# The front of a hybrid decoder step: where the squares of the first norm are summed, and the order of the first adaLN and weight loads

## The chip, the cores and the metric

The kernel runs on one core of one Trainium2 chip. The metric is the device time of one execution in microseconds (us); lower is better. The core's engines are TensorE (PE, matrix products), VectorE (DVE), ScalarE (ACT), GpSimd (POOL), and SyncE (SP), which issues most of the transfers between HBM and the on-chip memory. Each engine works off its own list of instructions in order, and they wait for each other by semaphores. Between SBUF (the on-chip memory) and PE's accumulators lies PSUM.

## The reference

One step of a trunk of two layers: an SSD (Mamba-2) layer, then a pooling layer, each with adaLN modulation, an RMS norm ahead and a residual add. 1024 prompt tokens and 8 x 8 sample tokens go through it together, 1088 tokens in all, in float32. What the change touches is the beginning: the norm and modulation of the first layer, and its first input projection.

```python
def rmsnorm(x, g):
    xf = x.astype(jnp.float32)
    return xf * lax.rsqrt(jnp.mean(xf * xf, axis=-1, keepdims=True) + EPS) * g.astype(jnp.float32)
...
    sc = jax.nn.silu(c.astype(jnp.float32))
    for i in range(DEPTH):
        mod = sc @ ada_w[i].astype(jnp.float32) + ada_b[i].astype(jnp.float32)
        shift, scale, gate = jnp.split(mod, 3, axis=-1)
        hn = (rmsnorm(x, norm_g[i]) * (1.0 + scale[:, None]) + shift[:, None]).astype(x.dtype)
        ...
    zxbcdt = h @ w_in
    z = zxbcdt[..., :D_INNER]
    xbc = zxbcdt[..., D_INNER:D_INNER + CONV_DIM].astype(jnp.float32)
    dt_raw = zxbcdt[..., D_INNER + CONV_DIM:].astype(jnp.float32)
```

## The kernel before

Activations lie transposed: channels on the 128 partitions, tokens along the free axis. So `x` is eight tiles `xs[k]` of 128 x 1088, one for each 128 of the 1024 channels. A row of up to 512 numbers fits one PSUM buffer, so tokens are cut into the three chunks of `CH`: 368, 368 and 352.

To keep float32 accuracy with fast products, a value is kept as a rounded `hi` and a rest `lo`, and a product is three: hi x hi, hi x lo, lo x hi (`mm1`, L189: L190, L191, L192). Products on unrounded float32 operands, such as those with the tile `ones`, are issued as one plain product.

The front (`setup` and `front`) does this:

- `setup` issues the loads on SP's queue: `ct` (the conditioning), the eight `x` tiles, then the constants `vec` and `kc`. It forms silu(c) in `scp`. `warm(62)` (L241 to L245) puts 62 products of `ones` by `ones` on PE, whose results nobody reads.
- `front` squares each `xs[k]` on ACT (L1403, L1407) into one of four `raw` buffers, and DVE adds the squares in `rst` (L1408). `ms_log` (L298) sums over the partitions, one product of `ones` (128 x 128) by a chunk of `rst` (L302), and takes the logarithm on ACT (L305, Ln); `rstd` (L318, Exp with -0.5) gives the inverse root.
- An adaLN step `ada_first(kt)` gives shift and scale of one channel tile. `ada_block` (L248) loads its slab of 1 MB in two halves (L257), multiplies it with `scp` in eight small products, four at a time side by side in strips of the array (L261, two records each), copies the result with ACT to `mp` (L266) and turns it with two products (L270); two DVE pieces (L280, L281) then give `shf` and `scl`.
- The first two column blocks of the input weights are loaded whole (`stream_raw`, L121) and split whole: ACT rounds 128 x 1024 numbers (L141), DVE forms the rest (L145).
- The loop over k: `modulate` (L320) scales `xs[k]` on DVE (L325), ACT adds the shift and rounds (`hh`, L331), DVE forms the rest (`hl`, L332), ACT adds the shift in place for the time-step projection (L333); the 64 sample tokens take five more small pieces. For k = 0 this goes in three chunks. Then PE has 18 products (two weight blocks, three chunks, three products each) in six open accumulators, and four strip products for `pdt` (L1443) with `wdt`. The adaLN steps 1 to 7 run inside the loop, two ahead.

After the loop `front` drains the accumulators, and the rest of the first projection follows (`wh`, `wl` are its split weights), then the pairs of blocks, the scan and the second layer.

The kernel is written in a framework with a scheduler: when the program is built, it merges what the Python code issues into one list for each engine by its own estimate of readiness. `keep_in_program_order` and `issue_after(i)` bind it: an instruction issued within `issue_after(i)` is not put ahead of `i`. Tiles of one tag share `bufs` buffers in turn, and the framework adds the waits. `Slots` hands out large SBUF buffers, which also hold the adaLN slabs.

Of the kernel before, what the change touches and what calls it, by code (L numbers as in the profile page):

```python
# [15 lines left out]
P = 128  # L16
# [83 lines left out]
class Build:  # L100
# [87 lines left out]
    def mm1(self, ps, w, k, act, ch, first, last):  # L188
        nc, (hi, lo), (ah, al), (a, n) = self.nc, w, act, ch  # L189
        nc.tensor.matmul(ps[:, :n], hi[:, k, :], ah[:, a:a + n], start=first, stop=False)  # L190
        nc.tensor.matmul(ps[:, :n], hi[:, k, :], al[:, a:a + n], start=False, stop=False)  # L191
        nc.tensor.matmul(ps[:, :n], lo[:, k, :], ah[:, a:a + n], start=False, stop=last)  # L192
# [9 lines left out]
    def setup(self):  # L202
# [4 lines left out]
        for k in range(8):  # L207
            t = self.slots.get("x")
            nc.sync.dma_start(t, io["xT"][k])
            self.xs.append(t)  # L210
        self.vec = cp.tile([P, V_N], F32, tag="vec", name="vec")
        nc.sync.dma_start(self.vec, io["vec"])
        self.kc = cp.tile([P, K_N], F32, tag="kc", name="kc")
        nc.sync.dma_start(self.kc, io["kc"])
        self.ident = self.kc[:, K_ID:K_ID + 128]
        self.ones = cp.tile([P, P], F32, tag="ones", name="ones")
        nc.vector.memset(self.ones, 1.0)

# [7 lines left out]
        self.warm(62)  # L226
# [12 lines left out]
        nc.gpsimd.memset(self.ctm, 0.0)  # L239

# [7 lines left out]
    def ada_block(self, src):  # L248
# [3 lines left out]
        for hh in range(2):  # L252
            if src is None:
                raws.append(self.stream_next_raw().rearrange("p a m -> p (a m)"))
            else:
                raws.append(self.slots.get("ada"))
                nc.sync.dma_start(raws[hh][:, :1024].rearrange("p (a b) -> p a b", a=4), src[:, 4 * hh:4 * hh + 4, :])  # L257
# [8 lines left out]
        nc.scalar.activation(mp, pm[:, :256], AF.Copy)  # L266
# [53 lines left out]
    def modulate(self, l, k, x, rst, hi, lo, a, n, t):  # L320
# [4 lines left out]
        nc.vector.scalar_tensor_tensor(out=t[:, :pn], in0=x[:, a:a + pn], scalar=self.scl[l][:, k, 8:9], in1=rst[:, a:a + pn], op0=ALU.mult, op1=ALU.mult)  # L325
# [4 lines left out]
        else:  # L330
            nc.scalar.activation(hi[:, a:a + pn], t[:, :pn], AF.Identity, bias=sh)  # L331
            last = nc.vector.scalar_tensor_tensor(out=lo[:, a:a + pn], in0=t[:, :pn], scalar=sh, in1=hi[:, a:a + pn].bitcast(F32), op0=ALU.add, op1=ALU.subtract)  # L332
            nc.scalar.activation(t[:, :pn], t[:, :pn], AF.Identity, bias=sh)  # L333
        if pn < n:
# [3 lines left out]
            eng.tensor_tensor(out=t[:, pn:n], in0=x[:, s], in1=rst[:, s], op=ALU.mult)  # L338
# [118 lines left out]
    def dt_phase(self, ps):  # L457
# [15 lines left out]
        nc.scalar.activation(an, self.vec[:, V_ALOG:V_ALOG + 1], AF.Exp)  # L473
        nc.vector.tensor_scalar(an, an, -1.0, None, op0=ALU.mult)
# [919 lines left out]
    def front(self):  # L1394

        nc, io, sl = self.nc, self.io, self.slots
        xs = self.xs
        wdts = sl.get("wdt")
        wdt = wdts[:, :256].rearrange("p (k m) -> p k m", k=8)
        nc.sync.dma_start(wdt, io["wdt"])  # L1400
        rst = sl.get("rst")
        with self.ln_set():
            nc.scalar.activation(rst, xs[0], AF.Square)  # L1403
            for k in range(1, 8):
                sq = self.raw_tile()
                for a, n in CH if k == 7 else ((0, TOK),):
                    nc.scalar.activation(sq[:, a:a + n], xs[k][:, a:a + n], AF.Square)  # L1407
                    nc.vector.tensor_tensor(out=rst[:, a:a + n], in0=rst[:, a:a + n], in1=sq[:, a:a + n], op=ALU.add)  # L1408
            for a, n in CH:
                self.ms_log(rst, rst, a, n, 1.0 / 1024, "mm", 3)  # L1410
                self.rstd(rst[:, a:a + n])
        self.ada_first(0)
        self.hn = []

        self.wslots = []
        lower = [self.stream_split(i, True) for i in range(2)]
        with self.tc.issue_after(self.sel):
            self.warm(8, "mm", 3)
        self.ada_first(1)
        ws = [self.wsplit.pop(i) for i in range(2)]  # L1420
# [3 lines left out]
        pdt = self.pp.tile([P, 512], F32, tag="tr", bufs=2, name="pdt")  # L1424
        for k in range(8):
            if k < 6:
                self.ada_first(k + 2)
            if k == 4:
                self.stream_split(2)
            if k == 6:  # L1430
                self.stream_split(3)
            hi, lo = sl.get("hh", F32R), sl.get("hl", F32R)
            for a, n in CH if k == 0 else ((0, TOK),):
                last = self.modulate(0, k, xs[k], rst, hi, lo, a, n, xs[k][:, a:a + n])
                if lower:
                    lower.pop(0)()
            self.hn.append((hi, lo))
            for i in range(2):
# [509 lines left out]
```

## Time and profile before

| | |
|---|---|
| time, median of 3 runs | 1591.16 us (1591.13 to 1593.46) |
| the profiled execution | 1591.15 us |
| its span, first to last instruction | 1589.0 us |
| records of instructions in it | 30720 |
| mean granted PE clock | 0.999 |

The profile is one execution. A record is one piece of work of an engine; a plain float32 product leaves two. A row of the timeline gives the start and length in us, the engine, the line of the kernel, the operation, what it writes and reads, shapes, the number of records merged in the row, and in brackets the idle time before it with what ended it. A row of a line's own view gives the least, median and largest length in ns, and the first and last start. In a row of stretches stand start and end, length, then for each engine its busy time and records, then the clock granted to PE, the share of the DMA engines and the GB/s. In the view of waits a row gives who waited for whom, the sum in us, the count and the longest.

### The profile page before, as it was taken

What the parts mean: (1) busy time and instruction counts of PE and PEld (TensorE: products, weight loads), DVE (VectorE), ACT (ScalarE), POOL (GpSimd) and SP (SyncE); (2) the same over time, 40 slices, a digit from 0 to 9 for tenths busy, and PEclk for the clock granted to TensorE, in tenths of its full rate; (3) what the DMA queues carried; (4) which work ended last, traced back from release to release, by engine and by line L of the source; (5) the groups of instructions that cost most, each with busy time, mean ns of one, the idle gap of its engine ahead of it and who ended that gap; (6) DMA issues with size and microseconds to landing.
All of it is one profiled execution on the core that took longest, in us unless ns stands there. A gap on an engine that the chain in (4) does not pass through costs nothing.

```text
span 1589.0 us, 30720 instructions
## 1 busy us (share of the span) xinstructions
PE 1568.2 (99%) x11946; PEld 1505.1 (95%) x11946; DVE 1301.7 (82%) x2152; ACT 790.1 (50%) x1512; POOL 525.5 (33%) x558
## 2 busy tenths in 40 slices
PE   9999999999999999999999999999999999999997
PEld 7899999999999999989999999999999999999997
DVE  6874889887899989889888858988889777667886
ACT  6663344466766666665456348433333233233373
POOL 0133456522331413141211232366666530000241
PEclk9999999999999999999999999999999999999999
DMA  9422232365555565679999432232333379565783
GB/s 356 167 101 101 80 112 84 111 194 173 161 179 165 162 209 167 212 259 297 311 332 320 164 127 69 85 121 100 117 115 115 104 250 365 140 180 178 163 172 117
DMA packets 122304, 275.57 MB, mean 173 GB/s; under 512 B 18192, under 2 KB 59312, under 8 KB 122160
## 3 DMA queue, kind: packets, MB, share of 16 engines
q1 hardware_dynamic: 118128, 260.90, 48.4%
q0 software_dynamic: 4032, 12.72, 4.7%
q8 instruction: 94, 1.54, 0.4%
q14 instruction: 50, 0.41, 0.1%
HBM read 201.12 MB, written 70.23 MB: 171 GB/s over the span
## 4 chain that ended last, share of the span: by engine, by line
PE 85%; DVE 6%; issue 3%; DMA 3%; ACT 2%; POOL 1%; SPq 0%; DVEq 0%; ACTq 0%; POOLq 0%
PE st L1070 11%; PE st L1072 11%; PE st L1071 11%; PE mm L190 10%; PE mm L191 10%; PE mm L192 10%; PE op L1289 2%; PE op L1291 2%; PE op L1290 2%; PE y L641 2%; PE S L619 2%; PE y L645 1%; PE am L261 1%; PE tr L580 1%; PE tr L577 1%
## 5 line engine op out<-in xcount | busy, mean ns | idle before, releaser
L1072 PE MATMUL st<-hh,w 128*128 128x272 f32 x832 | 240.2, 289 | 0.0
L1070 PE MATMUL st<-hh,w 128*128 128x272 f32 x832 | 240.0, 288 | 0.0
L1071 PE MATMUL st<-hl,w 128*128 128x272 f32 x832 | 240.0, 288 | 0.0
L1070 PE MATMUL st<-t,w 128*128 128x272 f32 x624 | 179.6, 288 | 0.0
L1072 PE MATMUL st<-t,w 128*128 128x272 f32 x624 | 179.5, 288 | 0.0
L1071 PE MATMUL st<-t,w 128*128 128x272 f32 x624 | 179.2, 287 | 0.0
L190 PE MATMUL mm<-hh,wh 128*128 128x368 f32 (+1 forms) x528 | 178.9, 339 | 0.0
L191 PE MATMUL mm<-hl,wh 128*128 128x368 f32 (+1 forms) x528 | 174.0, 330 | 0.0
L192 PE MATMUL mm<-hh,wl 128*128 128x368 f32 (+1 forms) x528 | 173.2, 328 | 0.0
L1070 PEld LDWEIGHTS st<-hh,w 128*128 128x128 f32 x832 | 156.7, 188 | 0.0
L1071 PEld LDWEIGHTS st<-hl,w 128*128 128x128 f32 x832 | 156.7, 188 | 0.0
L1072 PEld LDWEIGHTS st<-hh,w 128*128 128x128 f32 x832 | 156.5, 188 | 0.0
L182 ACT ACTIVATE w<-wr 128x512 fp32r<-128x512 f32 x104 | 64.9, 629 | 165.5 <-PE st L1072 134.2
L627 POOL TENSOR_TENSOR hd<-h,cd 128x256 f32<-128x256 f32 x56 | 46.1, 824 | 285.9 <-DVE h L628 135.6
L1289 PE MATMUL op<-b,w 128*128 128x272 f32 x448 | 129.4, 289 | 0.0
L1290 PE MATMUL op<-b,w 128*128 128x272 f32 x448 | 128.8, 287 | 0.2 <-DVE b L1218 0.2
L1291 PE MATMUL op<-b,w 128*128 128x272 f32 x448 | 128.9, 288 | 0.0
L190 PE MATMUL mm<-gh,wh 128*128 128x368 f32 (+1 forms) x372 | 125.3, 338 | 0.0
L192 PE MATMUL mm<-gh,wl 128*128 128x368 f32 (+1 forms) x372 | 122.4, 329 | 0.0
L191 PE MATMUL mm<-gl,wh 128*128 128x368 f32 (+1 forms) x372 | 122.2, 328 | 0.1
L1070 PEld LDWEIGHTS st<-t,w 128*128 128x128 f32 x624 | 117.6, 189 | 0.1
L1072 PEld LDWEIGHTS st<-t,w 128*128 128x128 f32 x624 | 117.3, 188 | 0.0
(310 smaller groups left out, 4596.9 us busy)
## 6 DMA issues: line engine op xcount, KB each, us to landing
wr<-win SPq DMA_DIRECT2D x48, 512.0 KB, 3.8
wr<-pin SPq DMA_DIRECT2D x32, 512.0 KB, 3.8
acb<-acd SPq DMA_DIRECT2D x60, 256.0 KB, 4.4
wr<-pout SPq DMA_DIRECT2D x28, 512.0 KB, 5.2
x<-x1d SPq DMA_DIRECT2D x24, 544.0 KB, 6.7
x1d<-x SPq DMA_DIRECT2D x22, 544.0 KB, 6.2
wr<-pout POOLq DMA_DIRECT2D x20, 512.0 KB, 6.0
x<-xT SPq DMA_DIRECT2D x16, 544.0 KB, 6.7
```

What stands on the lines that cost most here:

```text
L182: self.last_hi = self.nc.scalar.activation(hi, src, AF.Copy)
L190: nc.tensor.matmul(ps[:, :n], hi[:, k, :], ah[:, a:a + n], start=first, stop=False)
L191: nc.tensor.matmul(ps[:, :n], hi[:, k, :], al[:, a:a + n], start=False, stop=False)
L192: nc.tensor.matmul(ps[:, :n], lo[:, k, :], ah[:, a:a + n], start=False, stop=last)
L619: nc.tensor.matmul(S[:, 256 * i:256 * i + 256], Bt, xde.rearrange("p r q -> p (r q)"), start=True, stop=True)
L627: nc.gpsimd.tensor_tensor(out=hd, in0=h[-1], in1=cd.unsqueeze(2).to_broadcast([P, 4, 64]), op=ALU.mult)
L1070: nc.tensor.matmul(ps[c][:, :QUART], hi[:, k], xh[:, t], start=(k == 0), stop=False)
L1071: nc.tensor.matmul(ps[c][:, :QUART], hi[:, k], xl[:, t], start=False, stop=False)
L1072: nc.tensor.matmul(ps[c][:, :QUART], lo[:, k], xh[:, t], start=False, stop=(k == 3))
L1289: nc.tensor.matmul(ps[:, :QUART], hi[:, k], xh, start=k == 0, stop=False)
L1290: nc.tensor.matmul(ps[:, :QUART], hi[:, k], xl, start=False, stop=False)
L1291: nc.tensor.matmul(ps[:, :QUART], lo[:, k], xh, start=False, stop=k == 7)
```

## The change

Five things are done in the front, and nothing elsewhere.

1. The squares are no longer added on DVE. For each tile, PE multiplies `ones` with the three chunks of its squares and accumulates over the eight tiles in three PSUM buffers (`ms`). After each of the first seven sets of three products come three filling products, and the filling ahead of them is 48 instead of 62.
2. SP's loads stand in another order: the slab of adaLN step 0 ahead of the constants, then `kc`, `vec`, the first halves (k below 4) of the two first weight blocks, slab 1, the second halves, `wdt`, and the other slabs.
3. The first adaLN step stands behind the last set of sums in PE's list; Ln and Exp of the second and third chunk, and the splits, stand behind its `mp`.
4. The two first weight blocks are split in parts of 2, 2 and 4 of the eight k (`first_split`).
5. In the loop, k = 1 also goes in chunks, k = 0 takes its products chunk by chunk, the shift in place of x tiles 0 and 1 is moved behind an adaLN step of k = 1 (L1492), the `pdt` products of k = 0 go with those of k = 1, and the adaLN steps are placed by hand among the products.

PE's list at the beginning, before: `warm` is the filling, `ms` the three sums, `am` the adaLN step, `mm` and `hh` the first real product.

```order
L245 MATMUL warm_205<-ones 128x128 x62
L302 MATMUL ms_312<-rst_284,ones 128x368
L302 MATMUL ms_316<-rst_284,ones 128x368
L302 MATMUL ms_320<-rst_284,ones 128x352
L261 MATMUL am_328<-ada_324,scp 32x256 x4
L261 MATMUL am_328<-ada_326,scp 32x256 x4
L270 MATMUL am_328<-kc,mp_337 128x9 x2
L245 MATMUL warm_353<-ones 128x128 x8
L190 MATMUL mm_381<-hh_407,w_13_345 128x368
```

The same place now: the first two of the eight sets (`raw` holds the squares of one tile).

```order
L271 MATMUL warm_213<-ones 128x128 x48
L1436 MATMUL mm_277<-raw_281,ones 128x368
L1436 MATMUL mm_278<-raw_281,ones 128x368
L1436 MATMUL mm_279<-raw_281,ones 128x352
L271 MATMUL warm_286<-ones 128x128 x3
L1436 MATMUL mm_277<-raw_290,ones 128x368
L1436 MATMUL mm_278<-raw_290,ones 128x368
L1436 MATMUL mm_279<-raw_290,ones 128x352
L271 MATMUL warm_295<-ones 128x128 x3
```

Six more sets follow in the same form, the last without filling behind it, and then the adaLN step, the turn and the eight filling products as before. Three products of sums have become 24, and 62 filling products 48 + 21.

ACT's list between the first adaLN step's `mp` and the first `hh`, before:

```order
L266 ACTIVATE mp_337<-am_328 128x256
L141 ACTIVATE w_13_345<-wr_343 128x1024
L331 ACTIVATE hh_407<-x_177,shf_274 128x368 x2
L141 ACTIVATE w_15_350<-wr_348 128x1024
L333 ACTIVATE x_177<-x_177,shf_274 128x368 x2
```

And now, with the Ln (L1444) and Exp (L343) of the later chunks and the first parts of the split (L262):

```order
L291 ACTIVATE mp_362<-am_353 128x256
L1444 ACTIVATE rst_276<-mm_278,eps 128x368
L262 ACTIVATE w_12_372<-wr_203 128x256
L343 ACTIVATE rst_276<-rst_276 128x368
L262 ACTIVATE w_14_374<-wr_204 128x256
L1444 ACTIVATE rst_276<-mm_279,eps 128x352
L356 ACTIVATE hh_408<-x_177,shf_268 128x368
```

One long split has given way to five shorter pieces. A second place on ACT is that of the third adaLN step (`mp_525` is its copy, `x_177` and `x_179` the shifts in place, `hh_543` the rounding of tile 2); before, the steps' copies stood between the roundings of the tiles.

```order
L291 ACTIVATE mp_491<-am_482 128x256
L368 ACTIVATE hh_463<-x_179 128x64
L1492 ACTIVATE x_177<-x_177,shf_268 128x1024
L1492 ACTIVATE x_179<-x_179,shf_268 128x1024
L262 ACTIVATE w_12_372<-wr_203 128x256
L262 ACTIVATE w_14_374<-wr_204 128x256
L291 ACTIVATE mp_525<-am_516 128x256
L356 ACTIVATE hh_543<-x_181,shf_268 128x1024
```

The third step's copy now stands behind two whole shifts and two parts of the split. The diff, cut to its core:

```diff
@@ setup
+        self.adaq = []
+        self.ada_load(0)
+        self.kc = cp.tile([P, K_N], F32, tag="kc", name="kc")
+        nc.sync.dma_start(self.kc, io["kc"])
         self.vec = cp.tile([P, V_N], F32, tag="vec", name="vec")
         nc.sync.dma_start(self.vec, io["vec"])
...
+        self.wfirst = [self.wp.tile([P, 8, P], F32, tag="wr", bufs=3, name=self.name("wr")) for _ in range(2)]
+        self.first_load(0)
...
-        self.warm(62)
+        self.warm(48)
...
+    def ada_load(self, m):
+        for hh in range(2):
+            self.adaq.append(self.slots.get("ada"))
+            self.nc.sync.dma_start(self.adaq[-1][:, :1024].rearrange("p (a b) -> p a b", a=4), self.io["adaA"][0, m][:, 4 * hh:4 * hh + 4, :])
+    def first_load(self, k):
+        for i, t in enumerate(self.wfirst):
+            self.nc.sync.dma_start(t[:, k:k + 4], self.items[i][0][:, k:k + 4])
+    def first_split(self, raw):
+        self.wslots += [self.slots.get("w0", F32R) for _ in range(2)]
+        hi, lo = (t[:, :1024].rearrange("p (k m) -> p k m", k=8) for t in self.wslots[-2:])
+        def part(a, e):
+            self.nc.scalar.activation(hi[:, a:e], raw[:, a:e], AF.Copy)
+            return lambda: self.nc.vector.tensor_tensor(out=lo[:, a:e], in0=raw[:, a:e], in1=hi[:, a:e].bitcast(F32), op=ALU.subtract)
+        return hi, lo, part
...
@@ front
         with self.ln_set():
-            nc.scalar.activation(rst, xs[0], AF.Square)
-            for k in range(1, 8):
+            for k in range(8):
                 sq = self.raw_tile()
-                for a, n in CH if k == 7 else ((0, TOK),):
-                    nc.scalar.activation(sq[:, a:a + n], xs[k][:, a:a + n], AF.Square)
-                    nc.vector.tensor_tensor(out=rst[:, a:a + n], in0=rst[:, a:a + n], in1=sq[:, a:a + n], op=ALU.add)
-            for a, n in CH:
-                self.ms_log(rst, rst, a, n, 1.0 / 1024, "mm", 3)
-                self.rstd(rst[:, a:a + n])
-        self.ada_first(0)
+                for cs in ((c,) for c in range(3)) if k > 5 else ((0, 1, 2),):
+                    a, e = CH[cs[0]][0], sum(CH[cs[-1]])
+                    nc.scalar.activation(sq[:, a:e], xs[k][:, a:e], AF.Square)
+                for c, (a, n) in enumerate(CH):
+                    mm = nc.tensor.matmul(ms[c][:, :n], self.ones, sq[:, a:a + n], start=k == 0, stop=k == 7)
+                if k < 7:
+                    with after(mm.ins):
+                        self.warm(3)
+            with after(mm.ins):
+                self.ada_first(0)
+            for c, (a, n) in enumerate(CH):
+                with after(self.mp.ins) if c else contextlib.nullcontext():
+                    nc.scalar.activation(rst[:, a:a + n], ms[c][:, :n], AF.Ln, bias=self.eps, scale=1.0 / 1024)
+                    self.rstd(rst[:, a:a + n])
+                if c == 1:
+                    self.wslots = []
+                    firsts = [self.first_split(t) for t in self.wfirst]
+                    with after(self.mp.ins):
+                        lower = [f[2](0, 2) for f in firsts]
...
         for k in range(8):
...
-            for i in range(2):
-                for c in range(3):
-                    self.mm1(pst[i][c], ws[i], k, (hi, lo), CH[c], k == 0, k == 7)
+            for i, c in itertools.product(range(2), range(3)) if k else ((i, c) for c in range(3) for i in range(2)):
+                mm = self.mm1(pst[i][c], ws[i], k, (hi, lo), CH[c], k == 0, k == 7)
+                if (i, c) == ((0, 0) if k == 1 else (1, 0)) and k != 6:
+                    with after(mm.ins):
+                        m = next(ada, None)
+                        if m:
+                            self.ada_first(m)
+                    if k == 1:
+                        with after(self.mp.ins):
+                            for j in range(2):
+                                nc.scalar.activation(xs[j][:, :NP], xs[j][:, :NP], AF.Identity, bias=self.shf[0][:, j, 8:9])
+                            lower = [f[2](2, 4) for f in firsts]
```

75 lines of the change are left out of this document (42 added, 33 removed).

## The prediction

> **What bounds the kernel now.** I read the page's head, then the busy time by stretches for TensorE (PE), then the timeline of the first 70 us.
>
> ```profile
> span 1589.0 us, 30720 instructions
> PE 1568.2 (99%) x11946; PEld 1505.1 (95%) x11946; DVE 1301.7 (82%) x2152; ACT 790.1 (50%) x1512; POOL 525.5 (33%) x558
> ...
> 0.00:17.24 17.24, 16.18 (x124) 1.00 0.90 335
> 17.24:19.16 1.92, 1.92 (x8) 1.00 1.02 410
> 19.16:23.94 4.78, 3.75 (x37) 1.00 1.03 411
> 23.94:67.10 43.16, 42.02 (x349) 1.00 0.71 259
> 67.10:100.00 32.90, 32.90 (x218) 1.00 0.21 78
> 100.00:1589.00 1489.00, 1471.45 (x11218) 1.00 0.53 170
> ```
>
> The stretches give start:end, length, PE's busy time and records, granted clock, DMA share and GB/s. PE is busy 99% of the span, and from 67.1 us on it hardly waits. So the front (everything before 67.1) decides only when that long stream begins: a microsecond there is a microsecond of the total, if nothing later absorbs it. The four stretches of the front are the filling products with nothing to compute, the three sums (L302), the first adaLN step up to the first real product, and the loop over k.
>
> The order after the front is, engine by engine, the same as before but for small exchanges on ACT, DVE and SP up to some 110 us, where PE is full. Hence everything is settled by 67.1.
>
> **The old front.** DVE adds the squares as x arrives, and PE needs three products for the sums.
>
> ```profile
> 5.29 1.11 ACT L1403 ACTIVATE rst<-x 128x1088 f32<-128x1088 f32 x1 [0.76 <-DMA x<-xT]
> ...
> 15.23 1.30 ACT L1407 ACTIVATE raw<-x 128x368 f32<-128x368 f32 x3 [0.28 <-DMA x<-xT]
> 16.55 1.43 DVE L1408 TENSOR_TENSOR rst<-rst,raw 128x368 f32<-128x368 f32 x3
> 17.24 1.99 PE L302 MATMUL ms<-rst,ones 128*128 128x368 f32 x6
> ```
>
> Squares of the first tile start at 5.29, those of the eighth at 15.23: the loads set this pace, some 1.4 us a tile, and DVE's last additions end at 17.98, while the sums already run. PE's filling products end just then, so they cost nothing.
>
> **Term 1: the squares on PE.** The changed front has 48 filling products, then eight sets of three products of `ones` with a tile of squares, with three filling products between sets (21 in all), in this order on PE's one queue. Two prices are needed, and both have rows.
>
> ```profile
> 0.00:5.85 5.85, 4.79 (x22) 4.79 (x23) 1.00 0.64 199
> 5.85:17.24 11.39, 11.39 (x104) 11.36 (x102) 1.00 1.03 405
> L302 PE MATMUL ms<-rst,ones x6: 459/472/475, 17.2 to 18.8; 128*128 128x368 f32 x4, 128*128 128x352 f32 x2
> ```
>
> The first two rows are the filling products alone (L245): 62 products are 124 records, two each. The first 22 records take until 5.85, 0.218 us each, the other 102 take 11.39 us (the 104 counts two that reach in), 0.112 each, though the granted clock reads 1.00 in both. So 48 products, 96 records, end at 5.85 + 74 x 0.112 = 14.1 us. At that time seven of the eight tiles are already squared: the sums do not follow the loads, they start behind the filling.
>
> The third row is the nearest to the new products: same `ones`, same type, same width. Six records: the first starts at 17.24, the last ends at 17.24 + 1.99 = 19.23 and lasts 0.46, so it starts at 18.77; they are 0.307 apart, and a set of three costs 6 x 0.307 = 1.84 us. That is more than the 1.4 us in which a tile arrives, so PE never waits for a square. Eight sets: 14.7 us. Filling: 21 x 2 x 0.112 = 4.7 us. The sums end at 14.1 + 14.7 + 4.7 = **33.5 us**, and the first adaLN product can start 0.1 later, at 33.6, against 19.16 before: **+14.4 us**.
>
> DVE loses nine additions, 8.3 us of work, but that work lay beside the loads, so it pays nothing back. ACT's squares need one of four `raw` buffers, which PE now frees; square 5 goes out when set 1 is read, about four sets ahead, so no wait comes of it. A filling product waits for the one two sets back, long done: 0 us; at most, if it waited for the drain of the set before it, 0.47 - 0.31 = 0.16 each, 1.1 us in all.
>
> Here a page speaks for the change. The Trainium skill, "TensorE: Matmul & The Clock Gate" (Back-to-back issue gap), gives N/2.4 + 2.5 ns a product whatever the type, 0.156 us for 368 columns. That is a fourth of the 0.614 us of L302's two records, and the measurement decides; by the page 24 products would be 3.7 us and the total 1594.2. Its page "FP8 and Floating Point Precision" says that true FP32 goes through the array in four passes; with it the trace agrees.
>
> **Term 2: from the sums to the first real product.**
>
> ```profile
> 20.32 0.64 PE L261 MATMUL am<-ada,scp 128*32 128x256 f32 x8 [0.52 <-DMA ada<-adaA]
> 21.03 0.38 ACT L266 ACTIVATE mp<-am 128x256 f32<-128x256 f32 x1 [0.18 <-PE am L261]
> 22.65 1.12 DVE L325 SCALAR_TENSOR_TENSOR x<-x,scl,rst 128x368 f32<-128x368 f32 x2
> 23.29 1.12 ACT L331 ACTIVATE hh<-x,shf 128x368 fp32r<-128x368 f32 x2 [0.65 <-DVE x L325]
> 23.94 0.95 PE L190 MATMUL mm<-hh,w 128*128 128x368 f32 x2
> ...
> 34.92 1.07 PE L261 MATMUL am<-ada,scp 128*32 128x256 f32 x16
> 36.11 0.38 ACT L266 ACTIVATE mp<-am 128x256 f32<-128x256 f32 x1 [0.88 <-PE am L261]
> ```
>
> Before, the second half of the adaLN slab landed late: from 19.16 to `mp` 1.87 us. Both halves will have landed long ago, and then it takes 36.11 - 34.92 = 1.19: **-0.7**. From `mp` to the first product were 2.91 us; the chain is the same, but ACT now has five pieces between `mp` and `hh` (two Ln, one Exp, two quarters of the weight split), by the rows below about 0.5 + 0.45 + 0.45 + 2 x 0.42, with mp's 0.38 2.6 us. `hh` began 2.26 us after `mp`: **+0.3**. The first real product comes at 33.6 + 1.2 + 2.9 + 0.3 = 38.0 against 23.94, **+14.0**.
>
> ```profile
> 18.06 0.57 ACT L305 ACTIVATE rst<-ms,eps 128x368 f32<-128x368 f32 x1 [1.44 <-PE ms L302]
> 18.66 0.51 ACT L318 ACTIVATE rst<-rst 128x368 f32<-128x368 f32 x1
> 21.59 1.06 ACT L141 ACTIVATE w<-wr 128x1024 fp32r<-128x1024 f32 x1 [0.17 <-DMA wr<-win]
> 23.68 1.22 DVE L145 TENSOR_TENSOR w<-wr,w 128x1024 fp32r<-128x1024 f32 x1
> 24.82 1.11 DVE L332 SCALAR_TENSOR_TENSOR hl<-x,shf,hh 128x368 fp32r<-128x368 f32 x2
> 79.15 0.63 ACT L182 ACTIVATE w<-wr 128x512 fp32r<-128x512 f32 x1 [1.91 <-PE mm L191]
> ```
>
> No row has a quarter (256 columns) of a split: from 1.06 at 1024 and 0.63 at 512 I take 0.42, between 0.2 (nothing fixed) and 0.63.
>
> **Term 3: the loop over k.** The old loop lasts 43.16 us. What PE needs in it:
>
> ```profile
> 44.87:50.01 5.14, 5.14 (x47) 4.38 (x46) 4.55 (x10) 3.92 (x6) 0.00 (x0) 1.00 0.97 353
> 50.01:55.17 5.16, 5.16 (x47) 4.40 (x47) 4.42 (x9) 3.84 (x5) 0.00 (x0) 1.00 0.58 216
> 59.45:63.29 3.84, 3.84 (x27) 3.10 (x26) 3.81 (x7) 2.27 (x3) 1.40 (x1) 1.00 0.22 70
> 34.09 1.15 ACT L333 ACTIVATE x<-x,shf 128x1024 f32<-128x1024 f32 x1 [0.94 <-DVE hl L332]
> ```
>
> Behind PE's busy time stand those of the weight loads, DVE, ACT and GpSimd.
>
> A k with an adaLN step takes 5.15, one without 3.84, so a step is 1.31; 8 x 3.84 + 7 x 1.31 = 39.9. The old loop lost 3.3 us, all in its first 16 us. The new one has the same products, and loses again there: for k = 0, `hl` of the first part stands on DVE behind two quarters of a split and one more `x` part (0.42 + 0.42 + 0.56, then 0.55), which leaves PE waiting about 0.9 us; the first `hh` and `hl` of k = 1 about 0.5 each; the third adaLN step's `mp` stands on ACT behind two whole shifts of x (1.15 each, the row L333) and two quarters, about 1.0 us for PE; 0.3 at k = 2. Sum 3.2: **-0.1, say 0**; the bounds are -3.3 (nothing lost) and +3.0 (twice the loss). From k = 3 on PE has 5.15 us of products a k against some 4.5 of DVE and 3.9 of ACT, a whole weight split included, so it stays full.
>
> **Loads.** On SP's queue adaLN slab 0 now goes ahead of the constants, the first weights come in halves, `wdt` goes behind them, and the later slabs follow.
>
> ```profile
> 15.16 17.50 SPq L257 DMA_DIRECT2D ada<-adaA  x12
> 30.00:36.00 6.00, 1.00 1.03 404
> 36.00:39.40 3.40, 1.00 0.50 200
> ```
>
> The old queue issued twelve half slabs from 15.16 on, and the transfers ran at full share (1.03, DMA share the last but one number) until about 36. These bytes are the same, and PE now wants slab 1 only after 38 us: 0 us, with this delay as the cover. Without it a half slab that is late costs about the 0.52 above. What waits on SP behind them (the last three slabs, the third weights, the stores of `hn`) follows PE's progress, as before.
>
> **Sum.** 14.4 - 0.7 + 0.3 + 0 = +14.0 us. The profiled execution took 1591.15 (span 1589.0 and 2.15 around it), the median is 1591.16, so both give **1605.2 us**, 0.9% slower.
>
> **Rivals.** (A) A product of squares costs what a split product costs, one record.
>
> ```profile
> 67.58 0.33 PE L192 MATMUL mm<-hh,wl 128*128 128x368 f32 x1
> 67.74 0.33 PE L190 MATMUL mm<-hh,wh 128*128 128x368 f32 x1
> ```
>
> They start 0.165 apart, with the same width. Then 24 x 0.165 = 4.0 in place of 14.7: +3.3, 1594.5. Against: `ones` and `raw` have the type of L302's operands, which showed two records of 0.307. 4%; half of it within 0.2%, half just over.
>
> (B) The end, on the other side: PE waits later on things that do not move with the front, and they absorb the delay. After 100 us PE is idle 1489.00 - 1471.45 = 17.6 us; all of it absorbed gives 1591.15 + 14.0 - 17.6 = 1587.6. It decides for "not slower" from 10.8 us absorbed. Against: the waits are for work that itself follows PE:
>
> ```profile
> PE pl L190 <- ACT pz L940: 2.5, 1, 2.5
> PE y L674 <- DVE xbc L611: 1.4, 1, 1.4
> PE am L261 <- DMA ada<-adaA: 0.5, 1, 0.5
> ```
>
> The only DMA among them is in the front. 4%: faster 2, the same 2.
>
> (C) The loop loses nothing, because weights in parts and `x` in parts start it smoothly: -3.3, 1601.9. 22%. For it: the parts of k = 1 too. (D) It loses twice as much, since ACT's queue now holds the shifts of two k and the splits ahead of an adaLN step: +3.0, 1608.2. 18%.
>
> **Numbers.** Forecast 52%, own range 1603.5 to 1606.8. With C and D, both priced at their far ends, 1601.0 to 1608.5 leaves out A, B and the tails. Faster by over 0.2% (3.2 us, about what a measurement of this kernel can tell from no change) 0.02, within it 0.04, slower 0.94.
>
> **What would show it.** In the changed profile: the first product of squares at 14.1 us, 48 of their records 0.307 apart, and no wait of PE in that stretch; the first adaLN product at 33.6, the first split product at 38.0; the end of the loop (first product with `wh`) near 81 instead of 67.1; equal stretches behind it. If the squares' records are 0.165 apart, or start before the filling ends, term 1 is wrong; if the loop ends near 78 or 84, C or D.

## The result and the profile after the change

The changed kernel takes 1607.99 us (median of 5 runs, 1605.93 to 1608.74) against 1591.16 (5 runs, 1590.54 to 1593.46): a ratio of 1.0103, 95% interval 1.0089 to 1.0117. The prediction, 1605.2, is a ratio of 1.0088. The median lies 1.2 us above the forecast's own range (1603.5 to 1606.8) and inside the wider one (1601.0 to 1608.5), which it had opened for its rivals C and D. The profiled execution took 1605.93 us with a span of 1604.1; it is the fastest of the five.

PE's busy time by stretches, of the changed kernel. The cuts are at the first product of squares, the first adaLN product, the first split product, the end of k = 1, the end of k = 5, and the first product with `wh`.

```profile
0.00:13.36 13.36, 12.30 (x96) 1.00 0.86 323
13.36:32.77 19.41, 19.41 (x92) 1.00 0.96 369
32.77:36.82 4.05, 3.55 (x38) 1.00 0.52 156
36.82:50.90 14.08, 13.38 (x113) 1.00 0.66 214
50.90:75.41 24.51, 24.51 (x185) 1.00 0.56 184
75.41:83.09 7.68, 7.68 (x54) 1.00 0.00 0
83.09:1604.10 1521.01, 1505.60 (x11433) 1.00 0.52 168
```

The same view of the kernel before, cut likewise: k = 0 and 1, k = 2 to 5 and the rest; k = 6 and 7 take 7.68 in both. Three adaLN steps lie in the first row and four in the second, as in the changed kernel.

```profile
23.94:38.64 14.70, 13.56 (x114) 1.00 0.95 378
38.64:59.45 20.81, 20.81 (x189) 1.00 0.76 253
...
67.13:1589.00 1521.87, 1504.32 (x11433) 1.00 0.52 168
```

| | before | predicted | after |
|---|---|---|---|
| first product of sums or squares | 17.24 | 14.1 | 13.36 |
| first adaLN product | 19.16 | 33.6 | 32.77 |
| first split product | 23.94 | 38.0 | 36.82 |
| first product with `wh` | 67.13 | 81.2 | 83.09 |
| from there to the end of the span | 1521.87 | the same | 1521.01 |

The front costs 12.9 us up to the first split product, the loop another 3.1 (46.27 in place of 43.19: 3.7 more in k = 2 to 5, 0.6 less in k = 0 and 1), and 0.9 come back later: 15.1, the difference of the spans. The two larger numbers have different causes.

**The sums.** The three sums `ms` (`mm` in the rows) are PSUM tiles: PE's accumulators lie in PSUM itself. PE's timeline of the changed kernel, and a row of ACT's:

```profile
13.36 1.99 PE L1436 MATMUL mm<-raw,ones 128*128 128x368 f32 x6
15.19 0.83 PE L271 MATMUL warm<-ones 128*128 128x128 f32 x6
15.86 1.99 PE L1436 MATMUL mm<-raw,ones 128*128 128x368 f32 x6
```

```profile
15.45 1.11 ACT L1434 ACTIVATE raw<-x 128x1088 f32<-128x1088 f32 x1 [5.03 <-PE mm L1436]
```

A set starts every 2.50 us: 15.19 - 13.36 = 1.83 for its six records, 0.67 for the filling behind it. No PE row of this stretch has a bracket: PE waits for nothing, and ACT waits 5.03 us for PE to read a square. The squares follow PE, not the loads.

**The loop.** From k = 2 to 5 PE is busy in every microsecond (24.51 of 24.51) and yet takes 3.7 us longer than before. Here is PE's timeline of the changed kernel, in k = 3 and, from 73.65 on, at the end of k = 5:

```profile
58.29 0.62 PE L286 MATMUL am<-ada,scp 128*32 128x256 f32 x2
58.84 0.43 PE L190 MATMUL mm<-hh,w 128*128 128x352 f32 x1
59.20 0.64 PE L286 MATMUL am<-ada,scp 128*32 128x256 f32 x8
59.77 0.43 PE L191 MATMUL mm<-hl,w 128*128 128x352 f32 x1
...
60.28 0.63 PE L286 MATMUL am<-ada,scp 128*32 128x256 f32 x6
60.84 0.44 PE L190 MATMUL p<-hh,w 128*128 128x368 f32 x1
...
62.48 0.74 PE L1499 MATMUL pdt<-x,wdt 128*32 128x256 f32 x8
63.15 0.43 PE L190 MATMUL mm<-hh,w 128*128 128x368 f32 x1
...
73.65 0.63 PE L1499 MATMUL pdt<-x,wdt 128*32 128x256 f32 x6
74.22 0.61 PE L295 MATMUL am<-kc,mp 128*128 128x9 f32 x4
74.76 0.73 PE L1499 MATMUL pdt<-x,wdt 128*32 128x320 f32 x2
```

And the same groups in PE's timeline of the kernel before:

```profile
48.47 0.75 PE L1443 MATMUL pdt<-x,wdt 128*32 128x256 f32 x8
48.93 1.15 PE L261 MATMUL am<-ada,scp 128*32 128x256 f32 x16
50.01 0.44 PE L190 MATMUL mm<-hh,w 128*128 128x368 f32 x1
```

Read the starts, not the lengths. The strip products (128*32) of one adaLN step, 16 records, stand in three pieces here, which take 0.55 + 0.57 + 0.56 = 1.68 us up to the next product; the full-width products between and behind them take 0.26 to 0.36, where such a product otherwise takes 0.165. In the kernel before, `pdt` and the step stand as one group: 50.01 - 48.47 = 1.54 for both, where here `pdt` alone takes 0.67. Here a change of kind costs a few tenths each time, and PE counts as busy meanwhile. In k = 5 the selection products (L295, the turn of an adaLN step) cut `pdt` in two: 0.57 + 0.65 us for what takes 0.67; in k = 4 it is in two pieces as well.

Summed over k = 2 to 5, each record counted up to the start of the next, and the same number of records in both kernels: `pdt` goes from 2.04 us to 3.79, the split products from 12.98 to 14.33, the adaLN steps from 4.33 to 4.69, and the selection products from 1.46 to 1.70. So the three pieces of k = 3 are the smaller part. Most of it is that `pdt` no longer stands next to a step in any of the four k, and that more full-width products stand at a change.

### The profile page after: what moved, and what is told of

Same layout as the page of the kernel before. It is cut to its first block, busy times and chain, and to the rows that moved or that the text cites. A ratio compares the mean times of both kernels' runs of the same rounds, so it can differ in the third digit from the quotient of the medians.

```text
span 1604.1 us, 30836 instructions
## 1 busy us (share of the span) xinstructions
PE 1586.4 (99%) x12002; PEld 1514.5 (94%) x12002; DVE 1297.1 (81%) x2151; ACT 788.4 (49%) x1516; POOL 523.2 (33%) x558
## 4 chain that ended last, share of the span: by engine, by line
PE 88%; DVE 5%; issue 3%; ACT 2%; DMA 1%; POOL 1%; DVEq 0%; SPq 0%; ACTq 0%; POOLq 0%
PE st L1098 11%; PE st L1100 11%; PE st L1099 11%; PE mm L190 11%; PE mm L191 10%; PE mm L192 10%; PE op L1317 2%; PE op L1319 2%; PE op L1318 2%; PE y L669 2%; PE S L647 2%; PE am L286 2%; PE y L673 1%; PE tr L608 1%; PE tr L605 1%
```

## The experiments

Each ran beside runs of the kernel before on the same chip; ratios are to these. "Loop" is from the first split product to the first product with `wh`. The trace behind the loop lasts between 1520.8 and 1525.7 us in the profiled executions, whatever was changed ahead of it, so a step is judged by its stretch, and the time by its median.

**1. No filling between the sets** (`a_nofill`).

```diff
-                if k < 7:
-                    with after(mm.ins):
-                        self.warm(3)
```

> The changed kernel without the 21 filling products between the sets of squares. Theory P (PE's own queue sets the front: filling, then sets, then the adaLN step, at the prices of the records): a set of three products stays at 1.83 us, the gap of 0.67 us between sets goes seven times, so the first adaLN product comes 4.7 us earlier than in the changed kernel (32.8 to 28.1) and the time is 4.7 us lower, about 1603. Rival C (the clock needs the filling between the sets): the sets get slower, the time changes by less than 2 us. Rival S (the squares are late: ACT or the loads set the pace): the gaps stay as waits of PE, the time does not change.

1604.37 us (1603.44 to 1605.9), ratio 1.0083 (1.0068 to 1.0098), 3.6 below the changed kernel, where 4.7 were expected.

```profile
0.00:14.78 14.78, 13.72 (x97) 1.00 0.88 331
14.78:29.50 14.72, 14.72 (x50) 1.00 1.03 398
```

From the first product of squares to the first adaLN product it is 14.72 instead of 19.41: the 4.7 us of theory P, and a set stays at 1.84. Both rivals fall. But the same 48 filling products that took 12.30 us now took 13.72, with a granted clock of 1.00 both times, so the adaLN step came 1.4 later than expected.

**2. Rounded squares** (`a_round`), and **3. the squares alone on PE, in the kernel before** (`b_pesums`).

```diff
-        self.ones = cp.tile([P, P], F32, tag="ones", name="ones")
+        self.onr = cp.tile([P, P], F32R, tag="ones", name="ones")
+        self.ones = self.onr.bitcast(F32)
...
-                sq = self.raw_tile()
+                sq = self.gp.tile([P, 1115], F32R, tag="raw", bufs=4, name=self.name("raw"))
...
-                    mm = nc.tensor.matmul(ms[c][:, :n], self.ones, sq[:, a:a + n], start=k == 0, stop=k == 7)
+                    mm = nc.tensor.matmul(ms[c][:, :n], self.onr, sq[:, a:a + n], start=k == 0, stop=k == 7)
```

> The changed kernel with the squares and the ones rounded to the type of the split products (the squares lose the low bits of their mantissa; the rest is computed as before). Theory P: a product of squares is then one record of 0.165 us in place of two of 0.307, a set is 0.5 in place of 1.83 us, eight sets save 10.7 us, sums end near 21.5 and the time is 10.7 us below the changed kernel, about 1597. Rival S (the arrival of the squares sets the front, whatever a product costs): less than 3 us are saved. If a product costs the same as before in this type: no change.

```diff
-        self.warm(62)
+        self.warm(48)
...
-                    nc.vector.tensor_tensor(out=rst[:, a:a + n], in0=rst[:, a:a + n], in1=sq[:, a:a + n], op=ALU.add)
-            for a, n in CH:
-                self.ms_log(rst, rst, a, n, 1.0 / 1024, "mm", 3)
...
+                for c, (a, n) in enumerate(CH):
+                    mm = nc.tensor.matmul(ms[c][:, :n], self.ones, sq[:, a:a + n], start=k == 0, stop=k == 7)
+                if k < 7:
+                    with self.tc.issue_after(mm.ins):
+                        self.warm(3)
```

> The kernel before with the squares alone moved to PE as in the changed kernel: 48 filling products, eight sets of three sum products with three filling products between them; loads, splits and the loop's program text as before (the loop's order on PE shifts a little with it). Theory P (term 1 and the -0.7 of term 2): first adaLN product at 32.8 instead of 19.2 us, +13.6, -0.7 because adaLN's first slab has landed, loop near 43, so 12 to 14 us above the kernel before, 1603 to 1605. Rival B of the prediction (the delay is absorbed later): under 8 us.

Rounded: 1601.74 us (1600.03 to 1602.83), ratio 1.0062 (1.0045 to 1.0079). Squares alone: 1604.44 (1603.03 to 1605.6), ratio 1.0075 (1.006 to 1.009). Stretches of the rounded kernel (sums, and loop), and the longest of PE's waits in its loop (who for whom: sum, count, longest):

```profile
13.46:22.33 8.87, 8.87 (x70) 1.00 1.03 384
...
26.38:76.81 50.43, 47.08 (x349) 0.97 0.59 209
```

```profile
PE mm L191 <- DVE hl L358: 3.1, 2, 2.7
```

The stretch of the kernel with the squares alone from the first split product to `wh`:

```profile
39.48:80.47 40.99, 40.61 (x316) 1.00 0.50 180
```

Rounding takes 19.41 to 8.87, 10.5 us, as theory P has it: a rounded product is one record, an unrounded one two longer ones. Of these, 4.2 are lost again in the loop (50.43 against 46.27), with 3.1 us of waits for `hl` and a granted clock of 0.97; the time falls by 6.2, not 10.7. Ahead of the longest wait, three pieces of DVE took 2.30, 1.30 and 0.98 us instead of 1.27 and 0.21 while GpSimd was adding (runs 6 to 8 are on this); that they are the whole wait was not tried.

The squares alone move the first product with `wh` by 80.47 - 67.13 = 13.3, within the expected 12 to 14. The loop's 40.99 is below the expected 43 because the second adaLN step and part of the third stand ahead of it: the stretch before it lasts 6.74 (32.74 to 39.48) instead of 4.78.

**4. The squares back on DVE, the rest of the change kept** (`a_dvesums`).

```diff
-        self.warm(48)
+        self.warm(62)
...
+                    nc.vector.tensor_tensor(out=rst[:, a:a + n], in0=rst[:, a:a + n], in1=sq[:, a:a + n], op=ALU.add)
+            for c, (a, n) in enumerate(CH):
+                mm = nc.tensor.matmul(ms[c][:, :n], self.ones, rst[:, a:a + n], start=True, stop=True)
```

> The changed kernel with the squares added on DVE as in the kernel before (62 filling products, one set of three sum products), everything else of the change kept. It tells the part of the squares from the part of the loads, splits and order of the loop. If the squares alone cost the time: sums end at about 19.2 us, first split product at 23.3 (1.1 to mp, 2.9 from there), loop 43.2 as before, time 1590.5. If the loop loses 3 us by the order of its own instructions on PE: the loop lasts about 46, time 1593.5. If the loop lost in the changed kernel only because it starts 13 us late against the loads: loop under 44. If instead the loads now come too late for a loop that starts at 23 us: PE waits for DMA on ada or wr in the loop, loop over 47.

1595.55 us (1593.41 to 1601.25), ratio 1.0031 (1.0017 to 1.0044). The first split product comes at 23.65, the loop lasts 46.53:

```profile
23.65:70.18 46.53, 45.70 (x348) 1.00 0.67 246
```

So the loop loses 3.3 us without the squares too, as the theory of the order has it (about 46), and PE waits for no transfer in it. The two halves of the change add up: 13.3 (run 3) and 70.18 - 67.13 = 3.05 make 16.4, against 83.09 - 67.13 = 16.0.

**5. PE's groups held together** (`a_chain`).

```diff
-                mm = self.mm1(pst[i][c], ws[i], k, (hi, lo), CH[c], k == 0, k == 7)
+                with after(self.am.ins) if step and k > 1 else contextlib.nullcontext():
+                    mm = self.mm1(pst[i][c], ws[i], k, (hi, lo), CH[c], k == 0, k == 7)
...
+            if step and k > 1:
+                with after(dtm.ins):
+                    list(step)
```

> The changed kernel with PE's order held in the loop from k = 2 on: each adaLN step's eight products stand in one piece (in the changed kernel those of k = 3 stand in three), and the two selection products come behind the four pdt products, not among them. Nothing else is changed. Theory B (what the loop loses from k = 2 on are the ends of broken groups: a product of 32 output columns next to one of 128 costs more than two of a kind): k = 2 to 5 go from 24.5 us to about 21, time 3.5 us lower than the changed kernel. Rival Q (ACT's and DVE's queues lose it, as the prediction's case D has it): k = 2 to 5 stay within 1 us, PE shows waits where the breaks were, the time stays within 1 us.

1608.44 us (1607.11 to 1610.16), ratio 1.0108 (1.0093 to 1.0123): no gain. The stretch k = 2 to 5, and PE's waits in it:

```profile
51.33:75.88 24.55, 22.93 (x186) 1.00 0.55 188
```

```profile
PE am L295 <- ACT mp L291: 0.8, 1, 0.8
PE mm L191 <- DVE hl L369: 0.6, 2, 0.3
```

The pieces are gone, PE is busy 1.6 us less, and 1.6 us of waits stand in their place (0.3 of them for `hl` at L357). Theory B alone falls; Q's numbers come out. Two things are left. PE's 22.93 us are still 2.1 above the 20.81 of the kernel before: each step stands as one, but apart from `pdt`. And the waits have two sources. Those for `hl`, 0.2 to 0.3 each, are late hand-overs of DVE. The longest, 0.8 for `mp`, follows GpSimd's additions (65.52 to 69.40): ACT's copy `mp` stands behind a piece that waited for a slow piece of DVE. DVE's row, and two of ACT's:

```profile
66.92 1.33 DVE L367 TENSOR_TENSOR x<-x,shf 128x64 f32<-128x64 f32 x1
```

```profile
68.29 0.26 ACT L368 ACTIVATE hh<-x 128x64 fp32r<-128x64 f32 x1 [1.72 <-DVE x L367]
...
69.40 0.36 ACT L291 ACTIVATE mp<-am 128x256 f32<-128x256 f32 x1
```

This order with GpSimd held was not tried.

**6. The steps of k = 2 to 5 back behind `pdt`** (`a_early`), and **7. the same with GpSimd held** (`a_early_pool`).

```diff
+            if 1 < k < 6:
+                with after(dtm.ins):
+                    self.ada_first(k + 2)
...
-                if (i, c) == ((0, 0) if k == 1 else (1, 0)) and k != 6:
+                if (i, c) == ((0, 0) if k == 1 else (1, 0)) and k < 2:
...
```

> The changed kernel with the adaLN steps of k = 2 to 5 put back to the place they had before: directly behind the four pdt products, ahead of the products of their k, so that both groups of 32 output columns stand as one and each step is half a k earlier. The front up to k = 1 is that of the change. Theory B+L (from k = 2 the loop loses by groups that stand apart, and by steps so late that DVE and ACT hand over their parts late): k = 2 to 5 last about 20.8 us instead of 24.5, the loop 42.6 instead of 46.3, time 3.5 us below the changed kernel. Rival F (the loop loses because of what the front leaves to it: weights in parts, x shifted late, loads): k = 2 to 5 stay above 23.5 us, time within 1 us of the changed kernel.

1608.71 us (1608.0 to 1611.74), ratio 1.0106 (1.009 to 1.0122). The stretches of k = 2 and 3 and of k = 4 and 5, and PE's waits in them:

```profile
51.04:61.38 10.34, 10.34 (x94) 1.00 0.94 311
61.38:75.16 13.78, 11.07 (x97) 1.00 0.22 64
```

```profile
PE mm L191 <- DVE hl L369: 2.7, 2, 2.0
```

By its sum, 24.1, and its time the run came out as rival F says; by its stretches it did not. The first two k now take 5.17 each, the 5.15 of the kernel before, and over all four PE's work is 21.4 us instead of 24.5. What is left are 2.7 us of waits: something new holds DVE up. A row of DVE's timeline there, and the first of three such rows on GpSimd's:

```profile
66.19 1.29 DVE L369 TENSOR_TENSOR hl<-x,hh 128x64 fp32r<-128x64 f32 x1
```

```profile
65.76 1.64 POOL L1063 TENSOR_TENSOR sw<-wr 128x512 f32<-128x512 f32 x1 [64.71 <-DMA wr<-win]
```

A 64-column piece that takes 0.21 elsewhere (at 59.38 in this run) takes 1.29 beside a GpSimd addition, and PE waits 2.0 us for it. Run 7 adds one dependence to run 6:

```diff
-            nc.gpsimd.tensor_tensor(out=s[:, f], in0=z[:, f], in1=z[:, l], op=ALU.add)
+            ins = nc.gpsimd.tensor_tensor(out=s[:, f], in0=z[:, f], in1=z[:, l], op=ALU.add)
+            if self.loop_end:
+                self.tc.add_manual_dep(ins.ins, self.loop_end.ins.name, ..., reason="loop_end")
```

> The changed kernel with the adaLN steps of k = 2 to 5 directly behind pdt, and in addition GpSimd's three additions on weights, which ran at 65.7 to 71 us beside the loop, held until the loop's last modulation is done. Theory G (beside a GpSimd addition DVE's own instructions with two inputs take a microsecond longer, and PE waits for them): DVE's 128x64 pieces stay at 0.22 us, PE's 2.7 us of waits for hl at L369 go, the k = 3 and k = 4 that took 7.4 and 6.1 us come to 5.2, the loop is 43 instead of 46.0 us, time 3 us below the run without the hold. Rival L (the parts are late for other reasons, ACT's split ahead of them): PE's waits in k = 3 and 4 stay over 1.5 us, the loop above 45.

(The k of 7.4 and 6.1 us are k = 4 and 5, counted from 0.) 1605.67 us (1604.88 to 1608.37), ratio 1.0096 (1.0083 to 1.0109), 3.0 below run 6; the intervals of the two ratios overlap, so the stretches decide. DVE's timeline in the same place, and the stretch of k = 4 and 5:

```profile
64.99 1.28 DVE L350 SCALAR_TENSOR_TENSOR x<-x,scl,rst 128x1024 f32<-128x1024 f32 x1
66.19 0.22 DVE L369 TENSOR_TENSOR hl<-x,hh 128x64 fp32r<-128x64 f32 x1
```

```profile
61.38:73.13 11.75, 10.80 (x97) 1.00 0.41 114
```

The loop goes from 46.05 to 43.95: theory G holds for two thirds of the 3 us. PE's waits for this piece fall from 2.7 to 1.0 us; what is left goes with DVE's own order, since the `x` part of the next k stands ahead of the piece for which PE waits (64.99 ahead of 66.19).

**8. GpSimd held, the changed order kept** (`a_pool`): the last diff, alone, in the changed kernel.

> The changed kernel with nothing but GpSimd's three additions held until the loop's last modulation is done; the order on PE in the loop is that of the change, its groups broken as before. Theory B (in the changed kernel PE loses by the places of its groups, and the slow DVE pieces are hidden behind them): no wait of PE goes, k = 2 to 5 stay at 24 us or more (24.5 in the changed kernel), time within 1 us of the changed kernel. Theory G alone (the collision with GpSimd is what the loop loses): k = 2 to 5 come to 22 us, time 2 to 3 us lower.

1609.5 us (1606.32 to 1610.3), ratio 1.0103 (1.0086 to 1.0119), that of the changed kernel: nothing gained. The stretch k = 2 to 5:

```profile
51.60:76.14 24.54, 24.54 (x185) 1.00 0.53 187
```

It is 24.54 against 24.51, though DVE's piece (L369 at 67.29) takes 0.22, where it took 1.30 in the changed kernel. In the changed kernel itself the order on PE sets the loop; GpSimd's part shows only once the order is mended. (In the kernel before, the same additions run at 55.56 to 60.85 and slow pieces of DVE too, and PE does not wait for them.)

**9. Both taken back** (`a_dve_early`): the diffs of runs 4 and 6 together.

> The changed kernel with both taken back: squares added on DVE (62 filling products, one set of sums) and the adaLN steps of k = 2 to 5 directly behind pdt. What is left of the change are the order of the loads, the weight splits by parts, and the place of steps 1 to 3. Theory B+L: the loop is 43.5 us or less in place of 46.5, first product with wh at 67 us, time within 0.15% of the kernel before (1589.5 to 1593). Rival F: loop still 46, time 1595, as with the squares alone taken back.

1592.36 us (1589.9 to 1593.55), ratio 1.0003 (0.9994 to 1.0012). The time is in theory B+L's range. But the loop lasts 44.91, between the theories, and `wh` starts at 68.65, not 67. The place of the steps is worth 1.6 of the 3.3 us that run 4's loop loses. Of the other 1.7, 0.9 lie ahead of the fifth adaLN step (44.47 - 23.74 = 20.73, before 43.79 - 23.94 = 19.85) and 0.8 behind the start of the seventh (13.84, before 13.04). What causes them was not tried.

**10 to 12. Versions meant to beat both.** `a_best` is runs 2, 1 and 6 together with 20 filling products ahead of the sums; `b_best` is the kernel before with rounded squares on PE, 20 filling products and the first slab ahead; `b_slab` is the kernel before with only this slab moved. The filling in `a_best`, and the slab in `b_best` and `b_slab`:

```diff
-        self.warm(48)
+        self.warm(20)
...
+        self.ada0 = [self.slots.get("ada") for _ in range(2)]
+        for hh in range(2):
+            nc.sync.dma_start(self.ada0[hh][:, :1024].rearrange("p (a b) -> p a b", a=4), io["adaA"][0, 0][:, 4 * hh:4 * hh + 4, :])
```

> The changed kernel with squares and ones rounded to the type of the split products (the squares lose the low bits of their mantissa), 20 filling products instead of 48, none between the sets, and the adaLN steps of k = 2 to 5 directly behind pdt. Theory P (PE's queue is the whole price of the squares): PE is then free before each square comes, the sums end behind the last square at about 17.2 us, the first split product comes at 21.3 (23.94 in the kernel before), the loop lasts 43 and the time is about 2.5 us below the kernel before, 1588.5 to 1590. Rival C (PE waits between the sets, and its clock falls without filling): sets or the loop's first products at half speed, time above 1591.

> The kernel before with squares and ones rounded to the type of the split products (the squares lose the low bits of their mantissa) and summed on PE behind 20 filling products, none between the sets, and adaLN's first slab loaded right behind x; loop text as before. Theory P: sums end at 16.6 us, first adaLN product at 16.7 instead of 19.2 us, the loop's end (first product with wh) 2.5 to 3 us earlier than before, near 64.4, time 1588 to 1589. Rival D (the gain is lost in the loop to slabs and weights that land no earlier): wh near 67, time within 1 us of before.

> The kernel before with nothing but adaLN's first slab loaded right behind x, ahead of the constants. It prices the -0.7 of term 2 by itself. If the late half slab was the whole of it: mp 0.7 us earlier, wh 0.5 to 0.7 us earlier than 67.13, time 0.5 us lower, within 0.2% of before. Rival D: the constants and weights that now land later cost it again, wh at 67.1 or later.

In this order: 1592.94 us (1591.2 to 1599.57), ratio 1.0011 (0.9999 to 1.0023); 1591.34 (1589.08 to 1597.24), 1.0005 (0.9996 to 1.0015); 1593.18 (1591.15 to 1595.43), 1.0012 (1.0003 to 1.002). None is faster than the kernel before. Stretches of `a_best` (sums, loop), and the two longest of PE's waits in its loop:

```profile
8.49:16.69 8.20, 6.37 (x28) 1.00 1.00 395
...
21.24:67.59 46.35, 42.81 (x349) 1.00 0.73 264
```

```profile
PE mm L190 <- ACT hh L357: 1.3, 1, 1.3
PE mm L191 <- DVE hl L358: 1.1, 2, 0.8
```

The sums now end with the loads and the first split product comes 2.7 us earlier than before, at 21.24, where theory P expected 21.3. The loop then waits for ACT and DVE (in all it is 46.35 us long with 42.81 of work), and `wh` starts at 67.59 against 67.13. The time is in rival C's range, but its reason is not seen here: the granted clock reads 1.00 in these stretches. In `b_slab` the early slab is worth nothing: on ACT, `mp` stands behind the Ln and Exp of all chunks, and the first product waits for a whole weight split, which now stands behind the first `hh`. `wh` starts at 69.33, as rival D has it, but the first weights were not later: issued at 12.0 and landed 9.3 us after, where the kernel before starts its split at 21.59. Its loop lasts 44.47, at a granted clock of 0.96. Rows of PE's timeline:

```profile
21.43 0.61 PE L275 MATMUL am<-kc,mp 128*128 128x9 f32 x4 [0.95 <-ACT mp L271]
24.86 0.43 PE L190 MATMUL mm<-hh,w 128*128 128x368 f32 x1 [0.93 <-ACT w L141]
```

In `b_best` the same two waits stand ahead of the first split product (first adaLN product 17.21, first split product 23.72). Its loop can't tell rival D from P, since the clock fell in the profiled execution, one of the slower of its twelve (1595.58). Stretches of the sums and of the loop; the stretch between them reads 0.94:

```profile
7.09:17.21 10.12, 8.13 (x27) 0.70 1.01 391
...
23.72:70.11 46.39, 44.73 (x349) 0.93 0.67 243
```

Its four executions with a mean clock of 0.996 or 0.997 took 1589.08 to 1590.62 us, its three with 0.993 took 1595.18 to 1597.24. So part of what this version wins may be lost to the clock. Why it fell here and not in `a_best`, which has as little filling, is open.

## Why the prediction was right, and where it was not

**Term 1 (+14.4) held**, at +13.6. The set of 1.84 us was measured at 1.83, the filling between sets at 0.67, and no wait of PE came of the buffers or of the filling's own ones. Runs 1, 2 and 3 price it alone. Mis-sized was only the filling ahead: the 14.1 us for the end of 48 products took over the 22 slow records that the profile before has at its start. The changed kernel's has 14 and ended at 13.36, run 1's has 28 and ended at 14.78, so that 14.1 lay between was luck. Rival A (one record) fell: it is true of rounded operands (run 2), not of these. Two readings were wrong, and nothing hung on them: at 14.1 us six tiles are squared in the profile before, not seven, and DVE's nine additions are 9.2 us of work, not 8.3.

**Term 2: the -0.7 held, the +0.3 did not come.** From the first adaLN product to `mp` it is 1.14 us against 1.87, and from `mp` to the first split product 2.91 in both kernels: ACT's five pieces cost nothing. The early slab is less than half of the -0.7. In run 3 and in `b_slab`, where it has landed but the Ln and Exp of all chunks still stand ahead of `mp`, that first part takes 1.58 and 1.59; the other 0.4 go with the change's order on ACT.

**Term 3 is the step that failed**, by +3.1 where "say 0" stood. For k = 0 and 1 the amount was near and the reason was not. They lose 14.08 - (2 x 3.84 + 3 x 1.31) = 2.5 us where the working has 2.9 of waits; but PE waits there for 0.7 only, the other 1.8 are busy time, and the 1.0 that it feared for the third `mp` did not come. That amount is luck. For k = 2 to 5 it was wrong that "From k = 3 on PE has 5.15 us of products a k ..., so it stays full". PE did stay full, but 5.15 is not a price of the products: it is their price with `pdt` and adaLN standing as one unbroken group. k = 2 to 5 take 24.51 instead of 4 x 5.15 = 20.6, 3.9 lost without a wait. With the steps back behind `pdt` (run 6) PE's work there is 21.4 again. The order of the instructions is fixed when the program is built, so the place of the steps and the three pieces of k = 3 could be read beforehand; the working priced a step at 1.31 wherever it stands.

**Rival D came near in amount, not in its reason.** It had ACT's queue lose another 3 us. In the changed kernel PE waits in the loop for 0.7 us only, and the loss lies in k = 2 to 5, past the third adaLN step, ahead of which the two shifts stand. Something of D shows when the groups are held together (run 5): PE then waits, in part for an `mp` that ACT makes late; but by the rows shown there that wait goes back to a piece of DVE slowed beside GpSimd. That the scheduler broke the groups because it foresaw such waits is a guess, and not shown. Rival C (the loop loses nothing) fell; so did B, with 0.9 us given back behind the loop, less than the spread there.

**The loads** cost nothing, as predicted: PE waits for no transfer in the changed loop.

**The number.** The median lies 2.8 us above the prediction. 0.7 is that of the profiled run: the loop's 3.1, less 1.2 up to the first split product, less 0.9 behind the loop and 0.3 around the span. The working foresaw none of these four, so that they nearly cancel is luck too. The other 2.1 are the spread above this fastest run.

**Open.** With the squares and the steps both taken back (run 9) the loop still loses 1.7 us. Of the change this leaves the order of the loads, the splits by parts, the place of steps 1 to 3, and two things that the list of five leaves out: the diff also binds where the third and fourth weight splits and a small Exp (`an`) stand. None of these was taken back alone.

## What to carry to other kernels

An engine that is full is not an engine at its best: when a change scatters small products of another shape among large ones, compare starts with starts, because busy time counts the price of changing over as work here. Before work is moved to an engine that is already the bound, price the nearest row of the same operands, and then ask what a faster front would be given to: in `a_best` a front 2.7 us faster was lost again to waits in the loop. And read the printed order for broken groups before you price a loop by its steady state.

## What the runs showed of the hardware that was not expected

- Beside GpSimd's additions of two inputs, DVE's pieces with two inputs wait: 128x64 took 1.29 instead of 0.21 to 0.22 us, and the two runs that held GpSimd back (7 and 8) removed it. The Trainium skill, "SBUF — State Buffer" (Who interferes with whom), calls the port pair of the two engines an exclusive lock; the trace agrees.
- A group of products of 32 output columns that stands alone costs nearly the same for two records as for eight. Of an adaLN step, two records took 0.55 us up to the next product, six 0.56, eight 0.57, and sixteen in one piece 1.00.
- The granted clock fell for short stretches in some executions and not in others of much the same program, which makes some of the spread: to 0.91 from 700 to 720 us of the changed kernel, where the kernel before reads 1.00, and to 0.70 in the sums of `b_best`, where `a_best` reads 1.00.
- The same 48 filling products at the start took between 12.30 and 13.72 us in different executions, with a granted clock of 1.00 in the rows. The first 14 (changed kernel) to 28 (run 1) records start 0.21 us apart, the later ones 0.11; 14 x 0.1 is the difference. What sets their number stayed open.
